# Where the diagonal's score matmuls stand in a chunked recurrence, and how many key columns one tile of the levels holds

## The chip, the core and the metric

The kernel is one program on one NeuronCore of a Trainium2 chip. TensorE (PE) multiplies matrices into PSUM; its weight loads are listed on a row of their own, PEld. VectorE (DVE), ScalarE (ACT) and GpSimd (POOL) do the elementwise work, SyncE (SP) issues the DMAs. The metric is the device time of one execution in microseconds (us). Before the change it is 2663.89 us, the median of three runs.

## What is computed

The reference is one layer of an encoder over 2048 tokens of width 1024: a modulated layer norm, one input projection to 9216 columns, two mixers side by side, one output projection, and a residual with a second layer norm. The first mixer is a gated linear recurrence (HGRN2) with 8 heads of width 128, run forward and backward over the tokens; the second is neighbourhood attention over a grid of 32 x 64 tokens with 16 heads of width 64. The change concerns the recurrence:

```python
def step(state, xs):
    qc, kc, vc, dc = xs
    o = jnp.einsum('bhtd,bhdv->bhtv', qc, state)
    state = dc[..., None] * state + jnp.einsum('bhtd,bhtv->bhdv', kc, vc)
    return state, o
...
o = o_intra + jnp.moveaxis(o_inter, 0, 2)
```

Here k = 1 - f and the decay is the product of the gates f. The reference uses chunks of 32 tokens; inside a chunk it forms scores q * exp(b - b_mid) against k * exp(b_mid - b), keeps the causal half, and multiplies with v (`o_intra`). All inputs and outputs are float32.

## The kernel before

**Stages.** The kernel runs in five stages: a start (modulation, layer norm, transposes), attention of the first half of the tokens, the recurrence for both halves, attention of the second half, then the output projection. In all of them the input projections of a later unit are woven in between as dense work: each projection matmul (`proj_mm`, L278) has 128 key rows, 128 weight columns and 512 moving columns, and a dense step is three of them, one k of eight for one output tile. `weave` (L1316) hands out dense steps in proportion to the numbers that the mixer yields, so `yield 5` in `hgrn` means a certain number of projection matmuls between two pieces of recurrence. The tensor engine's order is the program's own (`tc.manual_schedule` with PE, L1356); the order on VectorE and ScalarE is set by the scheduler of the tile framework at compile time, from priorities in program order and a timeline of its own. Each engine then takes its queue in that order.

**The recurrence.** One call of `hgrn` (L419) is one head in one half of 1024 tokens: 8 heads x 2 halves make 16 calls, and each has two groups `g` of 512 tokens (four blocks `b` of 128). The kernel works with blocks of 128 tokens rather than 32. Scores inside a block come in three layers: the *diagonal* for pairs within the same 32 tokens (`diagonal`, L511), and two *levels*, w = 32 and w = 64 (`level`, L541), for pairs in neighbouring stretches of w tokens. Both directions are held in one matrix. For one group the pieces on the tensor engine are, in order:

- transposes of v (`turned`, L467, matmuls at L470), then of the decayed keys `de0` and `de1` (L470 again), each followed by the state updates (`updates`, L475, L478);
- the diagonal (L517): for each b and each of four stretches j of 32 keys, a weight tile of 32 columns of `kx`, first against 64 columns of `qx` and then, in a second pass, against 32. It writes the PSUM tile `pb`, at partitions j * 32. That is 32 matmuls per group, each recorded as two instructions;
- the levels (L545): for each of two w and four b, two weight tiles of 64 columns of `xk` against 64 columns of `xq`, into the PSUM tile `pa`. That is 16 matmuls per group, also two instructions each;
- the outputs (L569, L571): v against the finished scores `pm`, and the forward states against the decayed queries.

Between these stand dense steps, and after most yields a piece of the *tail* of the call before (`next(tail)`, `hgrn_tail`, L617): backward states (L637, L639 on VectorE, L643 on the tensor engine), the carried state of the second half (L666, L667), and the RMS norm of the outputs (L343 to L357, matmuls at L350 and L351).

**The other engines.** VectorE and ScalarE make the factors: `diagonal_factors` (L494; differences at L502, exponentials on ScalarE at L504 and L505, products at L506 and L508) and `level_factors` (L521; differences at L530 to L533, exponentials at L534 and L535, products at L536 to L538). `masked` (L548) copies `pa` out of PSUM on ScalarE (L551), takes the masked parts of the diagonal out of `pb` with three `copy_predicated` (L555), and adds them into the scores with four additions (L558). The outputs wait for these.

**Buffers.** `kx` and `qx` have one buffer each, so the factors of the next group wait until the diagonal has read them. `xk` and `xq` (tag `x`) have four for two levels, `pa` and `pb` one PSUM bank each, and `c`, the running sums of the gates, three for two directions.

Of the kernel before, what the change touches and what calls it, by code (L numbers as in the profile page):

```python
# [19 lines left out]
P = 128  # L20
# [18 lines left out]
def body(ctx: ExitStack, tc: tile.TileContext, t):  # L39
    nc = tc.nc  # L40
    dve, act, pool, pe = nc.vector, nc.scalar, nc.gpsimd, nc.tensor
# [46 lines left out]
    def nm(s):  # L88
        cnt[0] += 1
        return f"{s}_{cnt[0]}"  # L90

    def tl(tag, dt=F32, shape=None):
        if tag in cur["smap"]:
            tag = cur["smap"][tag]
            return sh.tile([P, 512], dt, tag=tag, name=nm(tag), bufs=SH[tag])
        return cur["pool"].tile([P, 512] if shape is None else shape, dt, tag=tag, name=nm(tag), bufs=cur["bufs"].get(tag, 1))
# [4 lines left out]
    def ps(tag="mx"):  # L101
        if tag == "pj":
            return pp.tile([P, 512], F32, tag=tag, name=nm("pj"))
        tag = cur["map"].get(tag, tag)
        return cur["psum"].tile([P, 512], F32, tag=tag, name=nm("ps"), bufs=cur["ps"][tag])
# [313 lines left out]
    def hgrn(u, half, st, tail):  # L419
# [8 lines left out]
        def rates(d, g):  # L428
            col = d * 8 + u
            e = zs[d, g]  # L430
            dve.tensor_scalar_min(e, e, ECAP)
            L = tl("g")
            act.activation(L, e, AF.Ln, bias=1.0)
            c = tl("c")
            act.activation(c, e, AF.Ln, scale=lbt[:, col:col + 1], bias=1.0)
            r = tl("g")
            act.activation(r, L, AF.Exp, scale=-1.0, bias=l1m[:, col:col + 1])
            dve.tensor_tensor(e, e, r, op=ALU.mult)
            for b in range(4):
                lo, hi = b * P, (b + 1) * P  # L440
                if d == 0:
                    sl = slice(lo, hi)
                else:
                    sl = slice(hi - 1, lo - 1 if lo else None, -1)
                dve.tensor_tensor_scan(c[:, sl], c[:, sl], L[:, sl], 0.0, op0=ALU.add, op1=ALU.subtract)
            return c, e

        def ends(d, g, c, k):
            last = 127 if d == 0 else 0
            ei = tl("ei")  # L450
            act.activation(ei, c, AF.Exp)
            dec = tl("dec", shape=[P, 4])
            dve.tensor_copy(dec, v4(ei, P)[:, :, last])
            decs[d, g] = dec
            if d == 1:
                dve.tensor_copy(decb_all[:, g * 4:g * 4 + 4], v4(ei, P)[:, :, last])
            qi = tl(f"qi{d}")
            dve.tensor_mul(qi, qs[g], ei)
            qibs[d, g] = qi
            de = tl("de")  # L460
            for b in range(4):
                sl = slice(b * P, (b + 1) * P)
                act.activation(de[:, sl], c[:, sl], AF.Exp, scale=-1.0, bias=c[:, b * P + last:b * P + last + 1])  # L463
            dve.tensor_mul(de, k, de)  # L464
            return de

        def turned(src, tag):  # L467
            pk = ps("tr")
            for b in range(4):
                pe.transpose(pk[:, b * P:(b + 1) * P], src[:, b * P:(b + 1) * P], ident)  # L470
            ke = tl(tag)
            act.activation(ke, pk, AF.Copy)
            return ke

        def updates(ke, v):  # L475
            pu = ps("pu")
            for b in range(4):
                pe.matmul(pu[:, b * P:(b + 1) * P], ke[:, b * P:(b + 1) * P], v[:, b * P:(b + 1) * P], start=True, stop=True)  # L478
            return pu

        def forward_states(g, pu):
            for b in range(4):
                bb = g * 4 + b
                if half == 0 and bb == 7:
                    sn = sfb[u]
                else:
                    sn = tl("Sf", shape=[P, P])
                if (0, bb) in S:
                    dve.scalar_tensor_tensor(sn, S[0, bb], decs[0, g][:, b:b + 1], pu[:, b * P:(b + 1) * P], op0=ALU.mult, op1=ALU.add)
                else:  # L490
                    dve.tensor_copy(sn, pu[:, b * P:(b + 1) * P])
                S[0, bb + 1] = sn

        def diagonal_factors(g, cs, ks):  # L494

            kx, qx = tl("kx", shape=[P, 1024]), tl("qx", shape=[P, 1024])
            kslot, q4 = [], kx.rearrange("p (n h c) -> p n h c", h=4, c=16)
            for d in range(2):
                kslot.append(q4[:, :, ::3, :] if d == 0 else q4[:, :, 2:0:-1, :])
                c = cs[d].rearrange("p (n h c) -> p n h c", h=2, c=16)  # L500
                mid = c[:, :, d:d + 1, 0:1] if d else c[:, :, 0:1, 15:16]
                dve.tensor_tensor(kslot[d], c, mid.to_broadcast([P, 16, 2, 16]), op=ALU.subtract)  # L502
            q3 = qx.rearrange("p (n h c) -> p n h c", h=2, c=32)
            act.activation(q3, kx.rearrange("p (n h c) -> p n h c", h=2, c=32)[:, :, ::-1, :], AF.Exp)  # L504
            act.activation(kx, kx, AF.Exp, scale=-1.0)  # L505
            dve.tensor_tensor(q3, q3, qs[g].rearrange("p (n o c) -> p n o c", o=1, c=32).to_broadcast([P, 16, 2, 32]), op=ALU.mult)  # L506
            for d in range(2):
                dve.tensor_tensor(kslot[d], kslot[d], ks[d].rearrange("p (n h c) -> p n h c", h=2, c=16), op=ALU.mult)  # L508
            return kx, qx

        def diagonal(kx, qx):  # L511
            pb = ps("pb")
            for b in range(4):
                for k0, n, dst in ((0, 64, b * 64), (32, 32, 256 + b * 32)):
                    for j in range(4):
                        o = (b * 4 + j) * 64
                        pe.matmul(pb[j * 32:(j + 1) * 32, dst:dst + n], kx[:, o + k0:o + k0 + 32], qx[:, o:o + n],  # L517
                                  start=True, stop=True, skip_group_check=True, tile_position=(0, j * 32))
            return pb
# [20 lines left out]

        def level(w, pa, xk, xq):  # L541
            for b in range(4):
                for s0 in (0, 64):
                    t0 = s0 if w == 32 else s0 ^ 64
                    pe.matmul(pa[s0:s0 + 64, b * P + t0:b * P + t0 + 64], xk[:, b * P + s0:b * P + s0 + 64],  # L545
                              xq[:, b * P + t0:b * P + t0 + 64], start=True, stop=True, skip_group_check=True, tile_position=(0, s0))

        def masked(pa, pb):  # L548

# [11 lines left out]
        def outputs(g, v, pm):  # L561

            po = ps("po")
            for b in range(4):
                sl = slice(b * P, (b + 1) * P)
                bb = g * 4 + b
                has_f = (0, bb) in S
                has_b = not (g == 1 and b == 3)
                pe.matmul(po[:, sl], v[:, sl], pm[:, sl], start=(b == 0), stop=not (has_f or has_b), skip_group_check=True)  # L569
                if has_f:  # L570
                    pe.matmul(po[:, sl], S[0, bb], qibs[0, g][:, sl], start=False, stop=not has_b, skip_group_check=True)  # L571
            os_[g] = po

        for g in range(2):
            v = turned(vts[g], "v")
            next(tail, None)
            cs, ks = {}, {}
            cs[0], ks[0] = rates(0, g)
            yield 5
            next(tail, None)  # L580
            cs[1], ks[1] = rates(1, g)
            de0 = ends(0, g, cs[0], ks[0])
            yield 5
            next(tail, None)
            ke0 = turned(de0, "ke")
            de1 = ends(1, g, cs[1], ks[1])
            kx, qx = diagonal_factors(g, cs, ks)
            yield 3
            next(tail, None)
            forward_states(g, updates(ke0, v))  # L590
            ke1 = turned(de1, "ke")
            yield 3
            next(tail, None)
            pu = updates(ke1, v)
            if g == 0:
                ub = tl("ub")
                act.activation(ub, pu, AF.Copy)
                ubs[g] = ub
            else:
                ubs[g] = pu  # L600
            pb = diagonal(kx, qx)
            lf = [(w, *level_factors(w, g, cs, ks)) for w in (32, 64)]
            yield 6
            next(tail, None)
            pa = ps("pa")
            for w, xk, xq in lf:
                level(w, pa, xk, xq)
            pm = masked(pa, pb)
            yield 5
            outputs(g, v, pm)  # L610
# [992 lines left out]
```

## Time and profile before

| what | us |
|---|---|
| runs | 2659.10, 2663.89, 2664.66 (median 2663.89) |
| the profiled execution: span from its first to its last instruction | 2662.0 |
| the profiled execution: device time | not listed apart from the runs |
| recurrence, first to last diagonal (L517) | 569.8 to 1702.3 |
| copy of the level scores (L551, ScalarE), one of 32 | 0.58 |
| additions into the scores (L558, VectorE), one of 128 | 0.28 |
| granted clock of the tensor engine, mean | 0.992 |

The page counts 17332 matmul instructions and as many weight loads. Names such as `ps` stand for tiles in PSUM, `pj` for a projection's PSUM tile; a row of the timeline gives start, length, engine, line, operation, result and operands, shape, and how many instructions in a row it merges. A shape such as 128*32 128x64 means 128 rows by 32 columns of weights and 64 moving columns. Matmul ends are modelled, so this text works with starts. An instruction's length overlaps the next one's on the same engine.

### The profile page before, as it was taken

How to read it: one execution, taken by the hardware profiler on the slowest of the kernel's cores; microseconds unless marked ns; L12 is line 12 of the kernel's file. 1: busy time of each engine (PE TensorE's matmuls, PEld its weight loads, DVE VectorE, ACT ScalarE, POOL GpSimd, SP SyncE). 2: the span in 40 equal slices, each digit the busy share in tenths (PEclk: the TensorE clock that was granted, in tenths of full speed). 3: DMA queues.
4: the chain of work that ended last, by engine and by line, in shares of the span. 5: the costliest groups of instructions: out<-in, count | busy, mean ns of one | idle time of the engine just before them, and what ended most of it. 6: DMA issues, size and time to landing. Idle time of an engine off the chain costs nothing.

```text
span 2662.0 us, 46086 instructions
## 1 busy us (share of the span) xinstructions
PE 2597.9 (98%) x17332; PEld 2155.3 (81%) x17332; DVE 1767.0 (66%) x4354; ACT 1418.7 (53%) x2808; POOL 105.8 (4%) x142
## 2 busy tenths in 40 slices
PE   6999999989999999999999999999999999999998
PEld 5888888878888888888888888887777777788887
DVE  7445545377777778877778877455777778648443
ACT  4534444376666667666666665354666667431110
POOL 0000000000000000000000000000000000032221
PEclk9999999999999999999999999999999999999999
DMA  7475454212111126212221122355444445444331
GB/s 268 140 212 146 132 172 157 91 45 72 60 64 64 60 76 226 80 37 76 76 76 64 56 79 77 100 159 143 125 130 128 131 129 154 107 153 132 95 95 56
DMA packets 225550, 295.94 MB, mean 111 GB/s; under 512 B 28599, under 2 KB 117431, under 8 KB 224183
## 3 DMA queue, kind: packets, MB, share of 16 engines
q1 hardware_dynamic: 225327, 293.00, 36.1%
q8 instruction: 136, 2.23, 0.4%
q14 instruction: 87, 0.71, 0.1%
HBM read 217.72 MB, written 66.99 MB: 107 GB/s over the span
## 4 chain that ended last, share of the span: by engine, by line
PE 74%; DVE 2%; DMA 1%; ACT 1%; issue 0%; SPq 0%; DVEq 0%; ACTq 0%
PE pj L278 40%; PE ps L1432 4%; PE ps L1433 4%; PE ps L1434 4%; PE ps L1066 3%; PE ps L1047 3%; PE pj L291 2%; PE ps L478 2%; PE ps L1003 1%; PE ps L1006 1%; PE ps L470 1%; PE ps L545 1%; PE ps L569 1%; PE ps L517 1%; PE ps L571 1%; PE ps L643 1%
## 5 line engine op out<-in xcount | busy, mean ns | idle before, releaser
L278 PE MATMUL pj<-h,wh 128*128 128x512 f32 x4000 | 1278.4, 401 | 4.2 <-ACT wh L803 1.9
L278 PEld LDWEIGHTS pj<-h,wh 128*128 128x128 f32 x4000 | 723.6, 188 | 163.9 <-issue 23.0
L278 PE MATMUL pj<-h,wl 128*128 128x512 f32 x2000 | 784.2, 392 | 0.0
L278 PEld LDWEIGHTS pj<-h,wl 128*128 128x128 f32 x2000 | 376.0, 188 | 83.1 <-DVE wl L779 0.4
L1020 ACT ACTIVATE pbuf<-pbuf,mx 128x480 f32<-128x480 f32 (+2 forms) x256 | 164.2, 642 | 156.3 <-DVE mx L1015 155.7
L1015 DVE CUSTOM_DVE_ANT_1 pbuf<-ps,bias 128x480 f32<-128x480 f32 (+2 forms) x256 | 143.7, 595 | 119.3 <-PE ps L1006 103.2
L291 PE MATMUL pj<-wh,h 128*128 128x256 f32 x1024 | 196.5, 286 | 2.8 <-ACT vt L297 2.5
L291 PEld LDWEIGHTS pj<-wh,h 128*128 128x128 f32 x1024 | 163.5, 192 | 7.4 <-ACT vt L297 3.2
L268 ACT ACTIVATE wh<-wr 128x512 fp32r<-128x512 f32 x192 | 120.3, 627 | 79.9 <-PE pj L278 72.2
L269 DVE TENSOR_TENSOR wl<-wr,wh 128x512 fp32r<-128x512 f32 x192 | 131.6, 686 | 44.5 <-ACT wh L268 43.4
L291 PE MATMUL pj<-wl,h 128*128 128x256 f32 x512 | 144.8, 283 | 0.0
L1053 ACT ACTIVATE pt<-ps 128x512 f32<-128x512 f32 (+1 forms) x128 | 68.9, 539 | 131.6 <-PE ps L1047 131.4
L1051 DVE COPY pt<-ps 128x512 f32<-128x512 f32 (+1 forms) x128 | 79.4, 620 | 66.7 <-PE ps L1047 66.2
L464 DVE TENSOR_TENSOR de<-e,de 128x512 f32<-128x512 f32 x64 | 44.3, 692 | 118.1 <-ACT de L463 118.1
L1047 PE MATMUL ps<-ident,pbuf 128*128 128x128 f32 x896 | 119.3, 273 | 0.7 <-DVE pbuf L1025 0.7
L1047 PEld LDWEIGHTS ps<-ident,pbuf 128*128 128x128 f32 x896 | 105.5, 141 | 16.5 <-ACT pbuf L1020 1.1
L1025 DVE TENSOR_SCALAR pbuf<-pbuf,mx 128x480 f32<-128x480 f32 (+2 forms) x256 | 108.5, 438 | 4.4
L752 ACT ACTIVATE e<-pj 128x512 f32<-128x512 f32 x98 | 58.4, 596 | 83.6 <-PE pj L278 77.2
L1408 ACT ACTIVATE yh<-yr 128x512 fp32r<-128x512 f32 x52 | 32.7, 629 | 130.0 <-PE ps L1433 113.0
L1481 DVE TENSOR_TENSOR vt<-ps,gt 128x512 f32<-128x512 f32 x24 | 16.5, 692 | 126.4 <-PE ps L1434 126.4
L291 PEld LDWEIGHTS pj<-wl,h 128*128 128x128 f32 x512 | 98.1, 192 | 1.4 <-issue 0.5
L1066 PE MATMUL ps<-pt,V 128*64 128x128 f32 x1376 | 95.5, 277 | 0.3 <-DVE pt L1051 0.3
(268 smaller groups left out, 4663.6 us busy)
## 6 DMA issues: line engine op xcount, KB each, us to landing
wr<-in_w_in SPq DMA_DIRECT2D x276, 256.0 KB
yr<-yq SPq DMA_DIRECT2D x64, 256.0 KB
V<-nv SPq DMA_DIRECT2D x248, 64.0 KB
bias<-tint SPq DMA_DIRECT2D x24, 480.0 KB
x<-in_x SPq DMA_DIRECT2D x32, 256.0 KB
ada<-in_ada_m SPq DMA_DIRECT2D x8, 1024.0 KB
wr<-in_w_v SPq DMA_DIRECT2D x32, 256.0 KB
nv<-vt SPq DMA_DIRECT2D x32, 256.0 KB
```

What stands on the lines that cost most here:

```text
L268: act.activation(hi, raw, AF.Copy)
L269: dve.tensor_tensor(lo, raw, hi, op=ALU.subtract)
L278: pe.matmul(pz, a, b, start=(k == 0 and n == 0), stop=(k == KT - 1 and n == 2))
L291: pe.matmul(pzs[tp][:, i * 256:(i + 1) * 256], a, b, start=(k == 0 and n == 0 and i == 0), stop=(k == KT - 1 and n == 2), skip_group_check ...
L1015: return dve.tensor_tensor_reduce(s[:, 0:nk].rearrange("p (r c) -> p r c", c=32), sc[:, 0:nk].rearrange("p (r c) -> p r c", c=32), bt[:, 0 ...
L1020: act.activation(s[:, 0:nk], s[:, 0:nk], AF.Exp, scale=-1.0, bias=mx[:, 0:1], accum_out=mx[:, 1:2])
L1025: dve.tensor_scalar(s[:, 0:nk], s[:, 0:nk], mx[:, 2:3], 1.0, op0=ALU.mult, op1=ALU.mult)
L1047: pe.transpose(ptp[:, c * P:(c + 1) * P], s[:, c * P:(c + 1) * P], ident)
L1066: pe.matmul(self.po[R][hs_, j * P:(j + 1) * P], self.st.V[c0 + c][:, j * P + hh * 64:j * P + hh * 64 + 64], pts[hh][:, c * P:(c + 1) * P], ...
L1432: pe.matmul(pz, yh[:, kk], wh, start=first, stop=False)
L1433: pe.matmul(pz, yh[:, kk], wl, start=False, stop=False)
L1434: pe.matmul(pz, yl[:, kk], wh, start=False, stop=last)
```

## The change

Two edits. In `level` a weight tile holds 32 key columns in place of 64, so there are four tiles per block in place of two, at partitions 0, 32, 64 and 96; the moving columns are the same 64 as before for both halves of a former tile. In `hgrn` the call of `diagonal` moves from behind the state updates to directly in front of the levels, behind `yield 6` and the piece of the tail. The results are the same scores in the same places of `pa` and `pb`.

```diff
         def level(w, pa, xk, xq):
             for b in range(4):
-                for s0 in (0, 64):
-                    t0 = s0 if w == 32 else s0 ^ 64
-                    pe.matmul(pa[s0:s0 + 64, b * P + t0:b * P + t0 + 64], xk[:, b * P + s0:b * P + s0 + 64],
-                              xq[:, b * P + t0:b * P + t0 + 64], start=True, stop=True, skip_group_check=True, tile_position=(0, s0))
+                for s0 in range(0, P, 32):
+                    t0 = b * P + (s0 // 64 if w == 32 else 1 - s0 // 64) * 64
+                    pe.matmul(pa[s0:s0 + 32, t0:t0 + 64], xk[:, b * P + s0:b * P + s0 + 32], xq[:, t0:t0 + 64],
+                              start=True, stop=True, skip_group_check=True, tile_position=(0, s0))
...
-            pb = diagonal(kx, qx)
             lf = [(w, *level_factors(w, g, cs, ks)) for w in (32, 64)]
             yield 6
             next(tail, None)
+            pb = diagonal(kx, qx)
             pa = ps("pa")
             for w, xk, xq in lf:
                 level(w, pa, xk, xq)
```

## Prediction

> **What bounds the kernel now.** I read the page from the top: the busy shares first.
>
> ```profile
> span 2662.0 us, 46086 instructions
> PE 2597.9 (98%) x17332; PEld 2155.3 (81%) x17332; DVE 1767.0 (66%) x4354; ACT 1418.7 (53%) x2808; POOL 105.8 (4%) x142
> ```
>
> The change touches the recurrence stage alone, so the table by stretch comes next, with one stretch laid over that stage. Its columns are length, then busy time and instructions of PE, PEld, DVE, ACT and POOL, the granted clock, the DMA share and GB/s.
>
> ```profile
> 537.00:1750.00 1213.00, 1196.96 (x8946) 1009.45 (x8945) 903.43 (x2197) 766.90 (x1418) 1.67 (x12) 0.99 0.24 79
> ```
>
> TensorE is busy for 1197 of 1213 us, VectorE for 903 (74%), ScalarE for 767 (63%), at a clock of 0.99 and with the DMA engines a quarter full. A busy TensorE need not be what sets the end, so the chain of waits inside the stage is next, here over 20 us of its steady part, and then the list of what TensorE waited for in the whole stage.
>
> ```profile
> by line: PE pj L278 79.7%; PE ps L478 8.9%; PE ps L545 5.4%; PE ps L517 4.2%; PE ps L470 2.2%
> ```
> ```profile
> PE ps L478 <- DVE Sf L489: 8.2, 1, 8.2
> PE ps L350 <- DVE rh L345: 4.5, 8, 1.4
> ```
> ```profile
> PE ps L569 <- DVE pm L558: 0.2, 1, 0.2
> ```
>
> The chain is TensorE from end to end. Its waits are few: one of 8.2 us at the stage's start, 4.5 us in eight waits of the tail's L350, 0.2 us for the outputs (L569), and nothing longer between; idle in all are 1213.00 - 1196.96 = 16 us. So the stage lasts as long as its list of matmuls, and whatever the edit saves or adds in that list shows in the end, unless a wait grows. The diagonal's matmuls (L517) and the levels' (L545) stand on the chain.
>
> **The change, part by part.** In one group (512 tokens of one head in one half: 8 heads x 2 halves x 2 = 32 groups) the diagonal follows the state updates (L478) and is followed by projection matmuls (L278); the levels stand about 7 us later between projection matmuls. TensorE's rows of one group, start and length in us, then count:
>
> ```profile
> 882.80 1.06 PE L478 MATMUL ps<-v,ke 128*128 128x128 f32 x8
> 883.70 0.60 PE L470 MATMUL ps<-ident,de 128*128 128x128 f32 x4
> ...
> 886.90 1.06 PE L478 MATMUL ps<-v,ke 128*128 128x128 f32 x8
> 887.89 0.91 PE L517 MATMUL ps<-qx,kx 128*32 128x64 f32 x64
> 888.73 0.73 PE L278 MATMUL pj<-h,wh 128*128 128x512 f32 x2
> 889.29 0.39 PE L278 MATMUL pj<-h,wl 128*128 128x512 f32 x1
> ...
> 894.06 0.39 PE L278 MATMUL pj<-h,wl 128*128 128x512 f32 x1
> 894.28 0.62 PE L278 MATMUL pj<-h,wh 128*128 128x512 f32 x2
> 894.74 0.39 PE L278 MATMUL pj<-h,wl 128*128 128x512 f32 x1
> 895.06 1.15 PE L545 MATMUL ps<-x,x 128*64 128x64 f32 x32
> 896.14 0.73 PE L278 MATMUL pj<-h,wh 128*128 128x512 f32 x2
> 896.70 0.40 PE L278 MATMUL pj<-h,wl 128*128 128x512 f32 x1
> ```
>
> *What the two bursts cost.* I measure from a start before a burst to a start behind it and take off the other matmuls, since starts are sounder than modelled ends. Three projection matmuls need 894.74 - 894.06 = 0.68, so two need 0.45. Levels: 896.70 - 894.74 - 0.68 = **1.28 us**. Eight updates need 883.70 - 882.80 = 0.90, so the diagonal costs 889.29 - 886.90 - 0.90 - 0.45 = **1.04 us**.
>
> *How much of that is work.* The weight loads show it, since their recorded starts have no modelled end. First the two bursts' load rows, then the min/median/max of one load:
>
> ```profile
> 887.89 0.79 PEld L517 LDWEIGHTS ps<-qx,kx 128*32 128x32 f32 x64
> ```
> ```profile
> 895.05 1.01 PEld L545 LDWEIGHTS ps<-x,x 128*64 128x64 f32 x32 [0.35 <-issue]
> ```
> ```profile
> L517 PEld LDWEIGHTS ps<-qx,kx x2048: 106/110/178, 569.8 to 1702.3; 128*32 128x32 f32 x187
> ```
> ```profile
> L545 PEld LDWEIGHTS ps<-x,x x1024: 132/138/138, 578.7 to 1709.6; 128*64 128x64 f32 x171
> ```
>
> Levels: the last load starts 1.01 - 0.138 = 0.87 after the first. Two tiles (of 64 key columns each) work side by side, so 32 instructions are 16 rounds, 58 ns each, 0.93 in all. Diagonal: 0.79 - 0.11 = 0.68 to the last load, 0.70 with it; four tiles side by side make 16 rounds, 8 with 64 moving columns and 8 with 32. If a 64-column round takes 58 ns here too, 8 x 58 = 0.47 leaves 0.23, or 29 ns, for each 32-column round: exactly half. So a round's time goes by its moving columns, not by how many tiles share it. The rest is switching: 1.28 - 0.93 = **0.35** for the levels and 1.04 - 0.70 = **0.34** for the diagonal. The row of the levels' loads shows where: the load unit sat 0.35 idle, "issue", ahead of the burst, and the first projection pair behind it needs 896.70 - 896.14 = 0.56 in place of 0.45.
>
> The Trainium skill says, in "TensorEngine Tiling (Array Packing)", section Key Properties, that a change of the tiling mode, though not a change of tile within a mode, drains TensorE; the trace agrees, with 0.34 and 0.35 us for a way in and out.
>
> *The levels with 32 key columns.* 16 matmuls of a group become 32, recorded as 64 instructions (each f32 matmul leaves two). Four tiles side by side make 64/4 = 16 rounds of 64 moving columns: as many as now and as long, 16 x 58 = 0.93. Bounds from rows: 64 x 11 ns (the diagonal's mean, 0.70/64) = 0.70, and 64 x 29 ns (the levels' present mean) = 1.86. I take 0.93, because 58 and 29 fit the diagonal's total. So smaller tiles give nothing by themselves; they put both bursts in one mode.
>
> *The diagonal's new place.* Its way out and the levels' way in merge: one switch in place of two, 0.34 or 0.35 saved. What is left at the old place is updates followed directly by projections. Rows of full-width f32 matmuls with that follower:
>
> ```profile
> 626.68 0.83 PE L643 MATMUL ps<-qi,Sb 128*128 128x128 f32 x6
> 627.26 0.70 PE L278 MATMUL pj<-h,wh 128*128 128x512 f32 x2
> 627.81 0.40 PE L278 MATMUL pj<-h,wl 128*128 128x512 f32 x1
> ```
>
> 627.81 - 626.68 = 1.13, and 6/8 of 0.90 plus 0.45 is 1.13: this exit costs nothing. Sum per group: 1.04 + 1.28 = 2.32 now; 0.70 + 0.93 + 0.35 = 1.98 after. That is 0.34, with the rounding of four starts **0.33 to 0.36**, x 32 = 10.6 to 11.5, say 11 us.
>
> *What moves with it.* The move issues no DMA and passes no DMA queue; on TensorE it passes the tail's matmuls (L643, L666, L350, L351) and six dense steps, which come earlier by its 1 us. The single buffers kx and qx come free about 7 us later, so the next group's factors (L502, L506, L508; L504 and L505 on ScalarE) start then. They are due at the next diagonal, on average (1702.3 - 569.8)/31 = 36.5 us after this one by the row of L517, so that is covered. The cover that gets thin is in front of the outputs (L569): the merges (L555), those factors and the level factors (L530 to L533) are now all released within 1 us.
>
> VectorE's rows of another group show what each of these takes:
>
> ```profile
> 854.54 0.31 DVE L555 COPY_PREDICATED pdb<-mskd,ps 128x128 f32<-128x128 uint32 x1 [0.71 <-PE ps L517]
> 854.74 1.29 DVE L502 TENSOR_TENSOR kx<-c 128x512 f32<-128x512 f32 x2
> 855.95 0.49 DVE L555 COPY_PREDICATED pdb<-mskd,ps 128x128 f32<-128x128 uint32 x2
> 857.22 1.23 DVE L506 TENSOR_TENSOR qx<-qx,q 128x1024 f32<-128x1024 f32 x1 [0.78 <-ACT qx L504]
> ...
> 861.53 0.42 DVE L530 TENSOR_TENSOR x<-c 128x256 f32<-128x256 f32 x1
> ...
> 864.22 1.17 DVE L558 TENSOR_TENSOR pm<-pdb 32x128 f32<-32x128 f32 x4
> ```
>
> Today the sums (L558) stand behind the eight level-factor steps (L530 to L533, twice). In the group of the first rows they are followed by the outputs like this:
>
> ```profile
> 898.72 1.17 DVE L558 TENSOR_TENSOR pm<-pdb 32x128 f32<-32x128 f32 x4
> ```
> ```profile
> 901.04 0.38 PE L569 MATMUL ps<-pm,v 128*128 128x128 f32 x2
> ```
>
> 898.72 + 1.17 = 899.89, so 1.15 us to spare. After, counted from the diagonal's end: first merge 0.2 (854.74 - 854.54), two L502 1.2 (855.95 - 854.74), two merges 0.5, the eight steps 2.7 (864.22 - 861.53), the sums 1.2: 5.8 us. The outputs come 0.93 + 0.1 + 4.9 (901.04 - 896.14) = 5.9 us behind that end. It fits, with 0.1 to spare if nothing else is put in front. Below, the loss is nothing (the sums go first); above, see the first rival. I take 1 us for the whole stage, since the nearest row, the 0.2 us that L569 waits today, is near nothing.
>
> The profiled execution's span of 2662.0 lies 1.9 under the median of the runs (2663.89; its own device time is not listed, and 2659.10 to 2664.66 is the spread). The saving is the same against both: 2663.9 - 11 + 1 = **2653.9, so 2654 us**.
>
> **The rivals.** *First, slower: VectorE's queue makes the outputs late.* Place: L558 ahead of L569. It decides once more than 0.1 us of other work stands ahead of the sums, and eats the saving at 0.1 + 0.34. L506 (1.2) could stand there, since its ScalarE step can be done by then: 1.1 late in a group like the one above. In the group of VectorE's rows the outputs leave more room:
>
> ```profile
> 867.39 0.61 PE L569 MATMUL ps<-pm,v 128*128 128x128 f32 x4
> ```
>
> 867.39 - 864.22 - 1.17 = 2.0 to spare in place of 1.15, so 0.2 late. The mean of 0.65 x 32 = 21 against 11 saved gives 2664 + 10 = 2674, and with a third of the groups spared 2667. With both L508 ahead as well (steps of L502's shape, so 1.2 more) it is 1.85 x 32 = 59 and 2712. For it: today's queue already puts the next group's work ahead of the sums. Against it: in program order the sums come ahead of those factors, VectorE is idle for 26% of the stage, and today's wait is 0.2 us in 32 groups. Chance 0.16.
>
> *Second, slower: the four tiles don't keep up over 128 instructions in a row.* Then the levels take up to 1.86 in place of 0.93: +0.93 - 0.34 = 0.59 x 32 = +19, 2683. It decides from 20 ns per instruction ((0.93 + 0.34)/64). Against it: the diagonal's 64 go at 11. Chance 0.04. The Trainium skill ("TensorE: Matmul & The Clock Gate", section Wait — 56ns, not 53.3ns?) states that matmul starts are never closer than about 25 ns; as an estimate from that page, 64 x 25 = 1.6 us for the levels and some 10 us more in all. The diagonal's row, 64 in 0.84 us, disagrees for tiles side by side.
>
> *Third, no change: nothing is merged,* because the drain belongs to something other than the mode (the new operands, say), or half the saving goes into new waits on the tail's L350, which waits 4.5 us already: 2659 to 2664. Chance 0.14.
>
> **How the numbers follow.** Forecast 0.66; third rival 0.14; first 0.16; second 0.04. The forecast's own range is 2650 to 2658. 0.2% (5.3 us) is about what a measurement of this kernel can tell from no change: faster 0.66, same 0.14, slower 0.20. Low end: 11.5 saved plus most of the 8.2 us of the start's wait, if VectorE's new order spares it: 2646. High end: the first rival in its milder form, 2667, and a little: 2671. What is left out is its costlier forms, the second rival and little below, under 0.2.
>
> **What would show it.** Right: one burst per group, 64 rows of the diagonal directly followed by 64 of the levels without idle weight loading between them, 1.98 us by the same differences of starts; no idle ahead of the old place's projections; busy times of VectorE and ScalarE unchanged. Wrong: the levels' part over 1.2 us; an idle stretch between the two; L569 waiting for L558, or L351 for L347, with tens of us in all.

## The result, and the profile after it

The changed kernel takes **2678.87 us**, the median of four runs (2677.3 to 2683.04), against 2662.11 for the kernel before in the same comparison: a ratio of 1.007, with a 95% interval of 1.0057 to 1.0083. It is slower by 0.7%, where 2654 was forecast. The profiled execution's span went from 2662.0 to 2677.0.

The page's busy line of the changed kernel first. TensorE's busy share fell from 98% to 97%, and no engine's busy time grew:

```profile
PE 2595.7 (97%) x18356; PEld 2144.4 (80%) x18356; DVE 1760.0 (66%) x4354; ACT 1413.0 (53%) x2808; POOL 105.6 (4%) x142
```

So the loss is idle time. To place it I take the output matmuls (L569) as milestones, 16 groups in each half of the tokens. The rows list all matmuls of that line in one half, with the start of the first and of the last. Before:

```profile
L569 PE MATMUL ps<-pm,v x128: 272/275/275, 585.3 to 1114.0; 128*128 128x128 f32 x128
L569 PE MATMUL ps<-pm,v x128: 272/275/348, 1149.4 to 1716.2; 128*128 128x128 f32 x128
```

After:

```profile
L569 PE MATMUL ps<-pm,v x128: 272/275/348, 585.3 to 1114.3; 128*128 128x128 f32 x128
L569 PE MATMUL ps<-pm,v x128: 272/275/377, 1149.4 to 1731.2; 128*128 128x128 f32 x128
```

The first half went from 528.7 to 529.0, the second from 566.8 to 581.8. The whole loss of 15 us lies in the second half. The stage's start, the way from one half to the other and everything behind the stage stayed as they were.

Did TensorE save what was promised? Its timeline in one group after the change:

```profile
860.34 0.39 PE L278 MATMUL pj<-h,wl 128*128 128x512 f32 x1
860.65 0.91 PE L517 MATMUL ps<-qx,kx 128*32 128x64 f32 x64
861.38 1.08 PE L545 MATMUL ps<-x,x 128*32 128x64 f32 x64
862.38 0.73 PE L278 MATMUL pj<-h,wh 128*128 128x512 f32 x2
862.96 0.39 PE L278 MATMUL pj<-h,wl 128*128 128x512 f32 x1
```

And its weight loads:

```profile
860.65 0.79 PEld L517 LDWEIGHTS ps<-qx,kx 128*32 128x32 f32 x64 [0.35 <-issue]
861.35 0.95 PEld L545 LDWEIGHTS ps<-x,x 128*32 128x32 f32 x64
```

Yes. By the prediction's own differences of starts the merged burst costs 862.96 - 860.34 - 0.68 = 1.94 us, where 1.98 was forecast. There is one idle of 0.35 ahead of it and none between its parts. The levels' 64 instructions take as long as their 32 did. Then what does TensorE wait for? Its waits in the stage:

```profile
PE ps L569 <- DVE pm L558: 11.1, 20, 1.9
...
PE ps L351 <- DVE rl L347: 6.9, 19, 0.7
PE ps L350 <- DVE rh L345: 5.4, 8, 2.3
```

The outputs waited 0.2 us before and wait 11.1 now, and the tail's norm waits 12.3 in place of 6.1. The list is short of the whole, since an idle time in it begins at the modelled end of the matmul ahead. The halves show the whole. Between a half's first and last output stand 15 bursts, so 15 x 0.34 = 5.1 us were to be saved in each: the first half lost 5.1 + 0.3 = 5.4 to waits and the second 5.1 + 15.0 = 20.1.

VectorE's rows in one group of the first half whose outputs wait, after the change:

```profile
895.28 0.43 DVE L337 TENSOR_SCALAR gt<-gt 128x512 f32<-128x512 f32 x1 [4.74 <-ACT gt L392]
895.62 0.31 DVE L555 COPY_PREDICATED pdb<-mskd,ps 128x128 f32<-128x128 uint32 x1
895.82 1.29 DVE L502 TENSOR_TENSOR kx<-c 128x512 f32<-128x512 f32 x2
...
897.42 0.42 DVE L530 TENSOR_TENSOR x<-c 128x256 f32<-128x256 f32 x1
...
898.76 0.68 DVE L395 TENSOR_TENSOR sg<-gt,gt 128x512 f32<-128x512 f32 x1
...
900.71 1.16 DVE L558 TENSOR_TENSOR pm<-pdb 32x128 f32<-32x128 f32 x4
```

TensorE in the same group:

```profile
901.04 0.39 PE L278 MATMUL pj<-h,wl 128*128 128x512 f32 x1
902.02 0.46 PE L569 MATMUL ps<-pm,v 128*128 128x128 f32 x2 [0.59 <-DVE pm L558]
```

Read the order on VectorE. It was idle for 4.74 us and took one gate step (L337). Then kx, qx and the x buffers came free within 1 us, as the parts of the burst ended, and what had waited for them was served ahead of the sums (L558): the next group's L502, its eight level differences, and with them one gate step (L395) of 0.61. The sums end at 901.87, when the outputs had been due at 901.27 (901.04 + 0.23), and the outputs start another 0.15 later. In the group of TensorE's rows above, the first of its head, L395 doesn't stand in between, and the outputs don't wait.

The second reader that is late is the tail's norm. In `hgrn_tail` only the calls of the second half have it, so the first half can lose nothing there. One place in the second half after the change, VectorE, then ScalarE, then TensorE:

```profile
1270.23 0.42 DVE L337 TENSOR_SCALAR gt<-gt 128x512 f32<-128x512 f32 x1
...
1274.43 0.40 DVE L345 CAST rh<-t 128x512 fp32r<-128x512 f32 x1
1274.75 0.68 DVE L395 TENSOR_TENSOR sg<-gt,gt 128x512 f32<-128x512 f32 x1
1275.35 0.68 DVE L347 TENSOR_TENSOR rl<-t,rh 128x512 fp32r<-128x512 f32 x1
```
```profile
1270.88 0.58 ACT L645 ACTIVATE t<-ps 128x512 f32<-128x512 f32 x1
1271.36 0.62 ACT L338 ACTIVATE gt<-gt 128x512 f32<-128x512 f32 x1
1271.88 0.62 ACT L433 ACTIVATE g<-e 128x512 f32<-128x512 f32 x1
1272.40 0.71 ACT L435 ACTIVATE c<-e,lbt 128x512 f32<-128x512 f32 x1
1273.02 0.62 ACT L343 ACTIVATE t<-t 128x512 f32<-128x512 f32 x1
```
```profile
1269.57 0.83 PE L643 MATMUL ps<-qi,Sb 128*128 128x128 f32 x6
...
1275.05 0.40 PE L350 MATMUL ps<-rh,ones 128*128 128x512 f32 x1
1276.09 0.50 PE L351 MATMUL ps<-rl,ones 128*128 128x512 f32 x1 [0.65 <-DVE rl L347]
```

The same place before the change, in the same order. The two matmuls of the norm stand 1272.38 - 1272.15 = 0.23 apart:

```profile
1264.07 0.42 DVE L337 TENSOR_SCALAR gt<-gt 128x512 f32<-128x512 f32 x1
```
```profile
1267.53 0.60 ACT L645 ACTIVATE t<-ps 128x512 f32<-128x512 f32 x1
1268.16 0.63 ACT L343 ACTIVATE t<-t 128x512 f32<-128x512 f32 x1
```
```profile
1266.66 0.83 PE L643 MATMUL ps<-qi,Sb 128*128 128x128 f32 x6
...
1272.15 0.40 PE L350 MATMUL ps<-rh,ones 128*128 128x512 f32 x1
1272.38 0.40 PE L351 MATMUL ps<-rl,ones 128*128 128x512 f32 x1
```

After it they stand 1.04 apart, so 0.81 is lost. The norm's square (L343) directly followed the copy L645 on ScalarE before (1267.53 and 1268.16). Now L338, L433 and L435 stand between, L338 because VectorE's L337 comes 3.3 us later than it did, counted from the tail's matmuls L643. Two more steps stand around L345 on VectorE: L445 ahead of it and L395 behind it. Why L337 is late shows in VectorE's busy time in a stretch around those L643, from 5.5 us ahead to 2.9 behind. The columns are length, then busy time of PE, PEld, DVE, ACT and POOL.

```profile
1264.08:1272.51 8.43, 8.43 (x42) 7.06 (x41) 8.43 (x22) 3.42 (x8) 0.00 (x0) 1.00 0.23 63
```

VectorE is busy for all of it. In the same stretch of the kernel before (5.7 ahead to 2.8 behind) it had slack, 7.30 of 8.46:

```profile
1261.00:1269.46 8.46, 8.46 (x44) 7.11 (x43) 7.30 (x21) 4.85 (x9) 0.00 (x0) 1.00 0.19 62
```

### The profile page after: what moved, and what is told of

Its sections match the earlier page's. It is cut to its first block, busy times and chain, and to the rows that moved or that the text cites. A ratio compares the mean times of both kernels' runs of the same rounds, so it can differ in the third digit from the quotient of the medians.

```text
span 2677.0 us, 48066 instructions
## 1 busy us (share of the span) xinstructions
PE 2595.7 (97%) x18356; PEld 2144.4 (80%) x18356; DVE 1760.0 (66%) x4354; ACT 1413.0 (53%) x2808; POOL 105.6 (4%) x142
## 4 chain that ended last, share of the span: by engine, by line
PE 66%; DVE 9%; ACT 3%; issue 1%; DMA 1%; SPq 0%; DVEq 0%; ACTq 0%
PE pj L278 33%; PE ps L1434 4%; PE ps L1432 4%; PE ps L1433 4%; PE ps L1066 3%; PE ps L1047 3%; PE pj L291 3%; PE ps L478 2%; PE ps L1003 1%; PE ps L1006 1%; PE ps L470 1%; PE ps L569 1%; PE ps L571 1%; DVE kx L502 1%; DVE pm L558 1%
```

## The experiments

**Theory A:** the saving on TensorE is real, and VectorE loses it again, because one burst frees the buffers of both kinds of factors at once. **Rivals:** the narrower tiles cost the time (B); TensorE's gain is lost at whichever reader comes next, whatever one does about a single one (C). Four kernels separate the edits. The table gives all ten, with the halves and the waits read as above (the halves from first to last output; waits in us, of the outputs and of the norm's L350 and L351 together). Ratios are against runs of the kernel before on the same chip; the median in its row is the one beside the changed kernel.

| kernel | median us | ratio (95%) | first half | second half | outputs wait | norm waits |
|---|---|---|---|---|---|---|
| before | 2662.11 | 1 | 528.7 | 566.8 | 0.2 | 6.1 |
| changed | 2678.87 | 1.007 (1.0057 to 1.0083) | 529.0 | 581.8 | 11.1 | 12.3 |
| e1_narrow | 2658.81 | 0.9991 (0.9981 to 1.0) | 527.9 | 563.8 | 0.2 | 5.5 |
| e2_move | 2679.67 | 1.0071 (1.0055 to 1.0086) | 530.2 | 582.0 | 7.1 | 12.5 |
| e3_sums_first | 2673.48 | 1.0047 (1.0031 to 1.0064) | 524.5 | 582.7 | 0 | 20.6 |
| e4_early | 2664.43 | 1.0014 (1.0005 to 1.0024) | 523.8 | 576.9 | 0 | 13.7 |
| e5_mix | 2654.57 | 0.9974 (0.9964 to 0.9983) | 523.8 | 563.7 | 0.2 | 5.7 |
| e6_after_less | 2664.72 | 1.0014 (1.0005 to 1.0023) | 528.9 | 571.4 | 11.0 | 5.6 |
| e7_before_less | 2659.66 | 0.9996 (0.9987 to 1.0006) | 528.7 | 567.4 | 0.2 | 7.2 |
| e8_seven_behind | 2670.74 | 1.004 (1.0026 to 1.0053) | 527.0 | 576.9 | 0 | 6.6 |
| e9_sums_first_less | 2652.63 | 0.9967 (0.9954 to 0.998) | 523.5 | 568.2 | 0 | 9.5 |
| e10_all_early | 2664.92 | 1.0011 (1.0002 to 1.0021) | 523.4 | 575.2 | 0 | 13.9 |

**e1_narrow: the tiles alone.** The kernel before with the new `level`; the diagonal stays.

```diff
-                for s0 in (0, 64):
+                for s0 in range(0, P, 32):
...
```

> The levels with 32 key columns alone; the diagonal stays behind the updates. Theory A (the narrow tiles cost TensorE nothing, the loss is in VectorE's queue behind the moved diagonal): no difference from before beyond 0.2%, 2657 to 2667; the levels' burst costs 1.25 to 1.30 us as before, outputs (L569) wait under 1 us in all. Theory B (twice as many level instructions are what costs): +17 us as in the changed kernel, 2675 to 2682.

Measured: 2658.81, hardly different from the kernel before. The levels' burst takes 1.24 us (from 891.55 to 893.47, less 0.68), a little less than the 1.28 of before. The narrower tiles cost nothing; B falls.

**e2_move: the move alone.** The changed kernel with levels of 64 key columns; the diff is against the kernel before.

```diff
-            pb = diagonal(kx, qx)
             lf = [...]
             yield 6
             next(tail, None)
+            pb = diagonal(kx, qx)
```

> The move alone; the levels keep 64 key columns. Theory A: TensorE loses the merged switch again, since a change from 32-column to 64-column tiles now stands between diagonal and levels, 0.1 to 0.3 us in 32 groups, and the waits of L569, L350 and L351 are the changed kernel's, some 37 us in all: 2680 to 2690. Theory B: back near the time before, 2659 to 2667.

Measured: 2679.67, as slow as the changed kernel and just under theory A's 2680; the move is what costs. Its burst shows what the narrow tiles are for:

```profile
858.22 0.39 PE L278 MATMUL pj<-h,wl 128*128 128x512 f32 x1
858.54 0.91 PE L517 MATMUL ps<-qx,kx 128*32 128x64 f32 x64
859.37 1.15 PE L545 MATMUL ps<-x,x 128*64 128x64 f32 x32
...
861.03 0.39 PE L278 MATMUL pj<-h,wl 128*128 128x512 f32 x1
```

861.03 - 858.22 - 0.68 = 2.13, so 0.19 more than with one width, which would be 6 us over 32 groups. The time doesn't show them: here the outputs come later and wait 7.1 in place of 11.1. Where TensorE waits for another engine, it is the other engine that sets the time.

**e3_sums_first: the order on VectorE.** The changed kernel, with the next group's factors queued behind the sums; TensorE's program is the same.

```diff
-                dve.tensor_tensor(v4(pm, P)[sl, :, sl], ...)
+                msk['sum'] = dve.tensor_tensor(v4(pm, P)[sl, :, sl], ...).ins
...
-            kx, qx = diagonal_factors(g, cs, ks)
+            with behind(): kx, qx = diagonal_factors(g, cs, ks)
...
-            lf = [(w, *level_factors(w, g, cs, ks)) for w in (32, 64)]
+            with behind(): lf = [(w, *level_factors(w, g, cs, ks)) for w in (32, 64)]
```

(`behind` is `tc.issue_after` of the last sum.)

> The changed kernel with one order set by hand: the next group's diagonal and level factors (L502, L530 to L533) are queued on VectorE behind the sums (L558). TensorE's program is the same to the instruction. Theory A: the waits of L569 fall from 16 us to under 2, those of L350 and L351 to about the 10 us of before or less, and the 12 us that TensorE saves show: 2646 to 2656. Rival C (VectorE has too much to do in the 12 us behind the levels, whatever the order): the waits only move to other lines, 2670 to 2685.

Measured: 2673.48. The outputs no longer wait, and the first half gains 4.2 us on the kernel before. The second half stays as slow as in the changed kernel, because the norm now waits 20.6 us:

```profile
PE ps L350 <- DVE rh L345: 13.4, 14, 1.6
PE ps L351 <- DVE rl L347: 7.2, 19, 0.7
```

So order explains the waits of the outputs, and C looked right for the second half.

**e4_early: merged at the other place.** Narrow levels moved forward to the diagonal's old place, the diagonal left there, masks and yields as in the kernel before. In program order the level factors now come ahead of the diagonal.

```diff
-            pb = diagonal(kx, qx)
             lf = [...]
-            yield 6
-            next(tail, None)
+            pb = diagonal(kx, qx)
             pa = ps("pa")
             for w, xk, xq in lf:
                 level(w, pa, xk, xq)
+            yield 6
+            next(tail, None)
             pm = masked(pa, pb)
```

> Diagonal and levels together, with 32-column tiles, but at the diagonal's old place directly behind the updates; the copy and the sums stay where they were in the program. The outputs then come some 7 us later behind the levels than in the changed kernel, so VectorE's queue has that much more room. Theory A: no waits of L569, the saving of TensorE in full: 2646 to 2654. Rival C: the crowd of work behind the levels makes other waits (L350, L351, L470), 2665 or more.

Measured: 2664.43, far above theory A's 2654 and just under C's 2665. In the first half the saving comes through whole: 523.8, which is 4.9 under the kernel before and 4.1 under e1_narrow, so over 15 distances between groups 0.27 each from the merge alone. The second half is 10 us longer than before; the norm waits 13.7 in place of 6.1.

**e5_mix: merge only where nothing takes it back.** Narrow tiles; in the first half as e4_early, in the second TensorE's order of the kernel before. The diff is against the changed kernel.

```diff
+            pb = diagonal(kx, qx)
+            if half == 0:
+                ...levels...
             yield 6
             next(tail, None)
-            pb = diagonal(kx, qx)
-            ...levels...
+            if half == 1:
+                ...levels...
```

> Tiles of 32 key columns everywhere. First half: diagonal and levels together at the diagonal's old place (behind the updates), masks and outputs where they were. Second half: the order of the kernel before. If the saving of the merged burst is real and is lost only where a wait takes its place, the first half runs at 69.9 us a head and the second at 75.3, and the time is that of the narrow tiles alone (2658.8) less 8 times 0.54, 2654.5 (2651 to 2657), faster than the kernel before. If what the early place gained in the first half was an accident of the whole order, the time is 2659 to 2664.

Measured: **2654.57**, where 2654.5 was expected, and faster than the kernel before by 0.26%. It is the fastest of the kernels that compute everything.

The halves take 523.8 and 563.7: e4_early's first and e1_narrow's second.

**e6_after_less and e7_before_less: less on VectorE.** The changed kernel and the kernel before, each without the products at L538, the levels' query factor times the query. VectorE's busy time falls by 32 us in the changed kernel (1760.0 to 1727.9 on its page). (One line less, so L558 and L569 are called L557 and L568 here.)

```diff
-            dve.tensor_mul(xq, xq, qs[g])
```

> The changed kernel without the two multiplications of a level's query factor by the query (L538), which leaves their part of the computation out: 64 times 0.68 us less on VectorE in the stage, and nothing less on TensorE. Theory A, VectorE's queue makes the outputs and the tail's norm late: the waits on L558 and most of those on L345 and L347 go, 15 to 30 us of the 37, and the time falls to 2649 to 2663. Theory B, the distance of five dense steps between the burst and the outputs is too short whatever VectorE has queued: less than 6 us go, 2673 to 2679.

> The kernel before with the same two multiplications left out. Theory A: VectorE had room there, its waits summed to 11 us, so 0 to 6 us go, 2656 to 2662, and the kernel without them after the change is no longer slower than this one. If VectorE's load bounds the stage in either order, this one falls by as much as the changed kernel does, and the distance of 17 us stays.

Measured: the changed kernel falls by 14 us to 2664.72, the kernel before by 1.2, which is within its interval. The distance of 17 us shrinks to 5. Theory A named 2649 to 2663 and so asked for a little more; what it got wrong shows in e6's list:

```profile
PE ps L568 <- DVE pm L557: 11.0, 20, 1.9
...
PE ps L350 <- DVE rh L345: 4.0, 8, 1.2
PE ps L351 <- DVE rl L347: 1.6, 7, 0.2
```

The norm's waits are back where they were before the change. Those of the outputs don't react at all: the steps that make them late (L502, L530 to L533, L395) stand ahead of L538 and are still there. These are two causes, not one.

**e8_seven_behind: more room for the outputs.** The changed kernel with the six dense steps ahead of the burst cut to four and the five behind it raised to seven.

```diff
-            yield 6
+            yield 4
...
-            yield 5
+            yield 7
             outputs(g, v, pm)
```

> The changed kernel with two of the dense steps (1.36 us) taken from ahead of the burst and put behind it: four ahead, seven between burst and outputs. All agree that the waits of the outputs on L558 go (16 us in the changed kernel). If they are the whole loss, the time is 2655 to 2662. If the tail's norm is a loss of its own, its waits on L345 and L347 stay in the second half at 15 us or more, and the time is 2664 to 2672.

Measured: 2670.74. The outputs' waits go, as all had said. The norm's fall to 6.6, against the second reading, which wanted 15 or more; yet the time is in its range, since a third wait appeared, for projection buffers that ScalarE empties (L392):

```profile
PE pj L291 <- ACT gt L392: 5.7, 1, 5.7
PE pj L278 <- ACT gt L392: 3.8, 12, 0.3
```

That one is 9.5 us. Why ScalarE is late there wasn't tried.

**e9_sums_first_less: both cures together.** The edits of e3_sums_first and e6_after_less in one kernel.

```diff
-            dve.tensor_mul(xq, xq, qs[g])
...
+            with behind(): kx, qx = diagonal_factors(g, cs, ks)
...
+            with behind(): lf = [(w, *level_factors(w, g, cs, ks)) for w in (32, 64)]
```

> The kernel of e3_sums_first, in which the next factors are queued behind the sums, with the multiplications L538 left out as in e6_after_less. Two causes that add up: the order on VectorE makes the outputs late (cured by the first edit), its backlog makes the tail's norm late (cured by the second). Then the waits on L558 stay away, those on L345 and L347 fall from 26 us to 8 to 14, and the time is 2653 to 2664, as fast as e7_before_less or faster. If there is one cause only, whose waits move to the next reader when they are cured in one place, the waits stay above 20 us and the time at 2668 to 2674.

Measured: 2652.63, a little below the range of the two causes and 7 us under e7_before_less, which leaves out the same work.

The two profiled executions lie 4.0 apart in their spans (2653.5 and 2657.5). The waits on the sums stay away, and the norm's fall from 20.6 to 9.5.

The halves say more than the total. In the first half the move is worth what TensorE saves: 523.5 against 528.7 in e7_before_less, 5.2 us where 15 x 0.34 are 5.1. C, taken as a law, falls there, as it did with e3_sums_first. In the second half it doesn't: 568.2 is no shorter than e7's 567.4. Against e6_after_less (571.4) only 3.2 us go, though the outputs' waits go whole, and the norm's listed waits are 9.5 there in place of 5.6. So even with less work on VectorE a part of the wait still moved on to the next reader.

**e10_all_early: is it the sums that delay the norm in e4_early?** As e4_early, with `masked` too ahead of `yield 6`.

```diff
+            pm = masked(pa, pb)
             yield 6
             next(tail, None)
-            pm = masked(pa, pb)
```

> As e4_early, with the masks and sums, too, at the diagonal's old place, directly behind the burst, so ahead of the tail's step. First half 69.9 us a head as before. If the second half of e4_early lost its saving because sums and tail's norm met in VectorE's queue, it falls from 76.7 to 74.5 to 75.3 us a head and the time to 2647 to 2656. If the norm is late because the factors have to be ready earlier, it stays at 76.5 or more, and the time at 2662 to 2668.

Measured: 2664.92, no better than e4_early. It isn't the sums. One group of its second half, on VectorE and then on TensorE:

```profile
1286.13 1.23 DVE L506 TENSOR_TENSOR qx<-qx,q 128x1024 f32<-128x1024 f32 x1
...
1291.55 1.36 DVE L445 TENSOR_TENSOR_SCAN c<-c,g 128x128 f32<-128x128 f32 x4
...
1294.69 0.68 DVE L667 TENSOR_TENSOR cl<-ps,cl 128x512 f32<-128x512 f32 x1
...
1296.23 0.42 DVE L345 CAST rh<-t 128x512 fp32r<-128x512 f32 x1
```
```profile
1286.86 1.02 PE L666 MATMUL ps<-cl,Sb 128*128 128x512 f32 x2
...
1296.70 0.50 PE L350 MATMUL ps<-rh,ones 128*128 128x512 f32 x1 [1.10 <-DVE rh L345]
```

The tail's matmul (L666) is done by about 1288, and VectorE takes its result (L667) only at 1294.69, behind the rest of the next group's factor work and, among others, L445. That queue is read from the rows; no run mended it there, so for this place the cause is argued and not shown.

## Why the prediction was wrong

- **TensorE's saving: right.** Forecast 1.98 us for the merged burst, measured 1.94; levels that take as long with four tiles as with two, measured; an old place whose exit costs nothing, no wait there. The second rival (tiles that don't keep up) and the first part of the third (nothing merged) are out.
- **"It fits, with 0.1 to spare if nothing else is put in front": the step that failed.** In 20 of 32 groups something else was in front: L395, 0.61 us, in six of the first half's sixteen and seven of the second's, and the norm's L345 and L347 in seven more of the second. In two further groups nothing was, and the outputs waited 0.15 all the same: the sums end at 1042.60, the outputs were due at 1042.59 and start at 1042.74. So the count of the steps was 0.1 too short, and the way from the sums' end to the outputs' start, 0.14 to 0.16 in all 22 groups that wait, wasn't in it. The prediction named L506 and L508 as the danger; both came behind the sums. It took 1 us of loss for the stage, "since the nearest row, the 0.2 us that L569 waits today, is near nothing". By gaps between starts L569 is 14.6 us late in all. The row of today stands for groups with mostly 1.15 us and more of cover, and says nothing of 0.1.
- **The reasons against the first rival were no reasons.** "In program order the sums come ahead": the queue on the chip had the next group's L502 and L530 to L533 ahead of them, and the kernel before already showed that order. "VectorE is idle for 26% of the stage": an average, while in the stretch of 8.43 us above it was idle for none, and in the group above for 0.04 from 895.28 to the end of the sums. The rival's own price (21 us of waits) came near the sum of the waits, 25.5 in the two halves, though only 14.6 of it lie at its place (0.75 in the group shown: 901.04 to 902.02, less 0.23).
- **The tail's norm: missed.** The prediction costed the moved factors as covered, since they are due 36.5 us later. That looks at their own reader only. The same batch stands in one queue with the norm's steps, and L350 comes 10 to 21 us behind the burst (1294.75 to 1304.68, and 1254.41 to 1275.05); in the second half this costs about 10 us more, the 20.1 less what the outputs lose there, 9.8. That "half the saving goes into new waits on the tail's L350" was said without a mechanism, and with a price of no change.

The cause, as e3_sums_first shows it for the outputs (in the first half the order alone brings 529.0 to 524.5) and e6_after_less for the norm (less work brings the second half from 581.8 to 571.4, where e7_before_less gains nothing): before the change two bursts 7 us apart freed two sets of buffers, and VectorE did the one set's work in the lull that followed the first (L502 at 854.74 and L530 only at 861.53 in the prediction's rows). With one burst the lull comes first and the work all at once behind it, in front of two readers. What stays open is the second half: e3, e4, e8 and e10 all lose there, and e9, with both cures, doesn't have TensorE's 5.1 us there either.

## What to carry to other kernels

When a matmul burst is moved, cost the moment at which it frees its buffers as carefully as the burst itself: list what is released then on the other engines, and who stands behind that in their queues. Cover counted to a tenth of a microsecond on a shared queue is no cover, and neither an engine's mean idle share nor program order says anything of the order that its queue really has. Where a saving is real in one stage and lost in another, as here in the two halves, apply the edit to the one.

## What the runs showed of the hardware

Changing between tiles of 32 and of 64 weight columns inside one burst costs time even without a full-width matmul in between: 2.13 against 1.94 us, of which about 0.05 is the narrow levels' own gain (e1_narrow's first half is 0.8 shorter than before, over 15 distances). The Trainium skill ("TensorEngine Tiling (Array Packing)", section Key Properties) states that a change of tiling mode drains TensorE; these rows agree, and put the change between two narrow modes at about 0.14 us, less than half of the 0.34 to and from full width.

A wait costs TensorE a little more than the list of waits gives it: 0.59 listed against 0.75 from start to start at 902.02, and 0.65 against 0.81 at 1276.09. The outputs start 0.14 to 0.16 us behind the end of the sums in each of the 22 groups in which they wait for them.
